# Where two norm-related steps stand among the matmuls of a hybrid decoder trunk: the first GLA head's key transposes, and the first token group's post-norm roots

## The chip, the cores and the metric

The kernel runs on one core of a Trainium2 chip. The metric is the device time of one execution in microseconds (us). Each run is timed on its own; several runs of one kernel give a median and a range. One further execution was recorded by the hardware profiler, and all rows below come from it.

## The reference, cut to what matters

The kernel computes a two-layer decoder trunk over 512 tokens and 16 meta tokens (528 columns) with a model width of 1024, all in float32. Each layer is a half-step SwiGLU feed-forward net, a token mixer, and a second half-step feed-forward net. Each is normed on its way in and again on its way out:

```
h = h + 0.5 * rmsnorm(swiglu(rmsnorm(h, g[0]), ...), g[1])
hn = rmsnorm(h, g[2])
mix = gla_mixer(hn, ...)      # layer 0; layer 1: swa_mixer(hn, ...)
h = h + rmsnorm(mix, g[3])
h = h + 0.5 * rmsnorm(swiglu(rmsnorm(h, g[4]), ...), g[5])
```

The mixer of layer 0 is chunked gated linear attention (GLA) with 4 heads of key width 128 and value width 256. Its part that the change touches, for one head:

```
chunk_kv = einsum('bhnsd,bhnsv->bhndv', kf * exp(b_last - bcum), vf)
S_next   = dec_c[..., None] * S + kv_c          # a scan over the chunks
o = o_intra + einsum('bhncd,bhndv->bhncv', q_dec, states)
```

The keys that go into the state, `kf * exp(b_last - bcum)`, have to be transposed on TensorE before the product with the values. The mixer of layer 1 is sliding-window attention. Between the layers one key/value set is computed from the normed residual.

## The kernel before, in words

Activations lie transposed: the 1024 channels are 8 tiles of 128 partitions, the tokens are columns. `H[:, k]` is tile k of the residual, `Y[:, k]` tile k of a sublayer's output. The columns are handled in two groups: group 0 has 272 columns (256 in layer 1), group 1 has 256.

A float32 product is made of three matmuls in a faster format: weight and activation are each split into a high and a low part, and high x high, low x high and high x low are summed (`mm3s`). Each weight tile of 128x512 thus needs one copy on ScalarE (ACT) and one subtraction on VectorE (DVE) before it can be used: `split_part`, with lines 226 and 227 in the profile. An activation tile is split in the same way: `build`, lines 398 (ACT) and 399 (DVE), gives the tile `x_<name>_k`.

What follows each sublayer is the same chain at six places, called by their names: `l0m` (after the first feed-forward net), `l0f1` (after GLA; the profile drops the last digit and writes l0f), `kv`, `l1m`, `l1f1` (l1f in the profile), `out`.

- `out_steps` computes the eight output tiles, for group 0 first and then for group 1 where the last tiles are concerned. A finished tile is added to `Y` (line 560 on DVE, or 558 on ACT), squared on ACT (`sq_post`, line 375; the first, and the last of group 1, straight into a sum, `acc_post`, line 372), and the squares are summed on POOL (line 376).
- Then `Residual.run` of that group starts as a job of its own. It waits `yield 1.8` and calls `roots`: two matmuls with a matrix of ones add the sums over the partitions (`st_post_<name><group>`, on TensorE, PE), ACT takes the reciprocal root (line 357) and a square (line 358), DVE refines it in three steps (lines 359 to 361).
- Then for each k, DVE multiplies by gain and root (line 437) and adds to `H` (line 438), ACT and DVE build `x_<name>_k`, ACT squares `H`. The roots of this pre-norm (`acc_<name>`, `R_<name>`) are applied later, to the product.
- `x_first` multiplies the new tiles with the next four weights: all k of group 0, then all k of group 1. `x_units` goes on with the other weights.

In GLA, `core(h)` is the job of one head. It runs while PE works through the `x` products of the other projections. In order: two scans on DVE, value transposes (`pv`, `pm`), decays `d`, the state's keys `f` (line 883 to 886, the last of which finishes them), keys `c` for the crossing chunk, `yield STATE_KEYS`, the transposes of `f` (`pk`), then the score products `pa` and `pb`, the states `ps`, the outputs `po` and `pn`, and a norm of its own (`st_go`).

The order of the work is set when the program is written. Jobs are generators; `Flow` holds a clock that only matmuls advance (`mm`: columns / 2400 for the fast format), and a `yield d` puts the job back until the clock has gone on by `d`. `mm3s` lets due jobs emit their instructions after each three matmuls. So a `yield` fixes behind which matmul a job's next instructions stand on PE, and among which others on ACT, DVE and POOL. On the chip each engine takes its instructions in this order and waits for data at the head of its own queue. One matmul with 272 columns advances the clock by 0.113, one with 256 by 0.107.

Of the kernel before, what the change touches and what calls it, by code (L numbers as in the profile page):

```python
# [40 lines left out]
START = 1.0  # L41
SECOND = 6.0
STATE_KEYS = 1.5
SCORE = 0.8
WIN = 2 * P + META
STAGGER = 5.0
# [78 lines left out]
def trunk_kernel(ctx: ExitStack, tc, a, out):  # L125
# [18 lines left out]
    def ps(name):  # L144
        return pp.tile([P, 512], F32, tag="ps", name=name)
# [203 lines left out]
    def roots(sums, n, c, name, dst=None, dim=D):  # L349
        s = ps(f"st_{name}")  # L350
        for i, t in enumerate(sums):
            mm(s[:, :n], ones, t[:, :n], i == 0, i == len(sums) - 1)
        yield SUMMED
        if dst is None:
            dst = (sums[1] if sums[1:] else acc_tile(f"root_{name}"))[:, :n]
        q, y = sums[0][:, :n], dst
        act.activation(y, s[:, :n], AF.Abs_reciprocal_sqrt, scale=1.0 / dim, bias=eps)
        act.activation(q, y, AF.Square, scale=dim ** -0.5)
        dve.scalar_tensor_tensor(q, s[:, :n], dim * 1e-6, q, op0=ALU.add, op1=ALU.mult)
        dve.tensor_scalar(q, q, -0.5 * c, 1.5 * c, op0=ALU.mult, op1=ALU.add)  # L360
        dve.tensor_tensor(y, q, y, op=ALU.mult)
        return y, s
# [57 lines left out]
    class Residual:  # L420
# [4 lines left out]
        def run(self, gi, g, sums):  # L425
            o, n = g
            nxt = self.nxt
            yield 1.8
            r, s = yield from roots(sums, n, self.c, f"post_{self.name}{gi}")
            if nxt is None:  # L430
                yield from self.store(gi, g, r)
                return
            for k in range(KD):
                h, y = H[:, k, o : o + n], Y[:, k, o : o + n]
                c = k % 2 * 256
                t = s[:, c : c + n] if n <= 256 else ps(f"t_{self.name}{gi}{k}")[:, :n]
                dve.scalar_tensor_tensor(t, y, self.gain(k), r, op0=ALU.mult, op1=ALU.mult)
                dve.tensor_tensor(h, t, h, op=ALU.add)  # L438
                nxt.build(gi, k)
                nxt.sumsq(gi, k)  # L440
                yield 1.0
            nxt.rjob[gi] = flow.spawn(nxt.factors(gi))
# [345 lines left out]
    def gla(x, finish):  # L788
        set_ahead(10)
        with tc.tile_pool(name="gp", bufs=1) as gp:  # L790
# [61 lines left out]
            def core(h, before):  # L852
# [39 lines left out]
                dve.tensor_tensor(kcv, kcv, blk(ks)[:, :, :64], op=ALU.mult)  # L892


                yield STATE_KEYS
                km = gp.tile([META, P], F32, tag="km", name=f"km{h}")
                p = ps(f"pk{h}")
                for b in range(3):
# [91 lines left out]
            for h in range(HEADS):  # L990
                cores.append(flow.spawn(core(h, [gate] + late + cores[h - 1 : h])))
                if h + 1 < HEADS:
                    kk = [("k", h + 1), ("q", h + 1), ("v", 2 * h + 2), ("v", 2 * h + 3)]
                    late = x_units(x, 4, L0, lambda i, g, p, kk=kk: evac(*kk[i], g, p))
# [71 lines left out]
    def swa(x, kv, finish):  # L1066
        kz, vt, vmz = kv
        set_ahead(10)
        with tc.tile_pool(name="ap", bufs=1) as ap:
# [25 lines left out]
            def soft(u, after):  # L1095
# [14 lines left out]
                for b in range(4):  # L1110
# [6 lines left out]
                    for e in range(2):  # L1117
# [3 lines left out]
                        )  # L1121
                    yield SCORE
                    for e in range(2):
# [242 lines left out]
```

## Time and profile before

| | |
|---|---|
| median of 3 runs | 1894.06 us (1893.08 to 1894.97) |
| the profiled execution, its time | 1895.05 us |
| the profiled execution, its span | 1893.3 us |
| mean granted TensorE clock | 0.995 |
| busy: PE / DVE / ACT / POOL | 1860.3 / 1356.2 / 1004.4 / 322.1 us |
| chain that ended last, PE's share | 84% |

The span runs from the first to the last recorded instruction; 1.75 us of the profiled execution's time lie around it. That execution took 0.99 us longer than the median. A row of the timeline gives a start in us from the span's start, a busy time in us, the engine, the line, the operation and the tile that it writes, and how many instructions stand together in the row; in square brackets stands how long the engine sat idle before it and which instruction ended that wait. The list of waits adds up these brackets by pair.

### The profile page before, as it was taken

The page shows a single profiled execution, that of the slowest core. Times are in us where ns is not written, and L with a number is a line of the kernel's source. Part 1 is how long each engine was busy: PE and PEld are TensorE (multiplying, and loading weights), DVE is VectorE, ACT ScalarE, POOL GpSimd, SP SyncE. Part 2 cuts the span into 40 slices and gives each one's busy share as a digit, 9 for nine tenths or more (in the row PEclk, how much of TensorE's full clock was granted, in tenths as well). Part 3 has the DMA queues.
Part 4 walks back from the last instruction along what each step waited for, and adds up shares of the span by engine and source line. Part 5 has one row for each costly group of instructions (what it writes and reads, how often), then busy time and mean ns, then how long its engine had stood idle before and what let it go on. Part 6 is the DMA issues. An engine that isn't in the chain of part 4 may idle for free.

```text
span 1893.3 us, 36987 instructions
## 1 busy us (share of the span) xinstructions
PE 1860.3 (98%) x14238; PEld 1775.4 (94%) x14238; DVE 1356.2 (72%) x2681; ACT 1004.4 (53%) x2181; POOL 322.1 (17%) x378
## 2 busy tenths in 40 slices
PE   8999999999999999999999999999989999999997
PEld 8999999998999999999999898989967898989897
DVE  6884848776574977484878775858788588858484
ACT  6662626563545665362655563636546566626363
POOL 2101010310001310101033001010353231010102
PEclk9999999999999999999999999999999999999999
DMA  5655556322123255555642456566321215565651
GB/s 192 151 153 138 151 145 168 106 71 72 49 65 104 68 134 156 141 153 139 169 148 57 106 153 154 151 150 171 109 67 35 79 46 127 155 153 156 151 146 45
DMA packets 133104, 231.17 MB, mean 122 GB/s; under 512 B 14912, under 2 KB 27584, under 8 KB 132928
## 3 DMA queue, kind: packets, MB, share of 16 engines
q1 hardware_dynamic: 111904, 190.94, 31.9%
q0 software_dynamic: 20736, 37.76, 12.8%
q8 instruction: 111, 1.82, 0.4%
q14 instruction: 65, 0.53, 0.1%
q10 hardware_dynamic: 288, 0.13, 0.0%
HBM read 226.67 MB, written 2.10 MB: 121 GB/s over the span
## 4 chain that ended last, share of the span: by engine, by line
PE 84%; DVE 11%; ACT 3%; issue 1%; DMA 0%; POOL 0%; SPq 0%; DVEq 0%; ACTq 0%; POOLq 0%
PE y L162 29%; PE a L162 21%; PE x L162 13%; PE c L162 10%; PE d L162 5%; DVE H L438 1%; PE o L162 1%; DVE w L227 1%; PE e L162 1%; PE po L162 1%; ACT w L226 1%; PE sc L162 1%; DVE x_l0m L399 1%; DVE x_l1f L399 1%; PE ps L162 0%
## 5 line engine op out<-in xcount | busy, mean ns | idle before, releaser
L252 POOL DMA_DIRECT2D raw<-in_w_in x144 | 125.7, 939 | 971.2 <-DMA raw<-in_w_in 331.6
L247 DVE TENSOR_TENSOR w_s<-raw,w_s 128x512 fp32r<-128x512 f32 x288 | 194.9, 688 | 105.6 <-ACT w_s L246 103.9
L162 PE MATMUL y<-hidl0f,w 128*128 128x256 f32 (+1 forms) x2112 | 260.5, 285 | 0.0
L162 PEld LDWEIGHTS y<-hidl0f,w 128*128 128x128 f32 x2112 | 258.7, 188 | 0.2
L227 DVE TENSOR_TENSOR w<-raw,w 128x512 fp32r<-128x512 f32 x378 | 242.9, 672 | 20.9 <-ACT w L226 18.9
L162 PE MATMUL y<-hidl1f,w 128*128 128x512 f32 (+1 forms) x1344 | 249.3, 346 | 0.5 <-ACT hidl1f L380 0.5
L162 PEld LDWEIGHTS y<-hidl1f,w 128*128 128x128 f32 x1344 | 212.2, 188 | 34.1 <-ACT hidl1f L380 1.3
L246 ACT ACTIVATE w_s<-raw 128x512 fp32r<-128x512 f32 x288 | 177.7, 625 | 108.2 <-DVE raw L262 67.7
L226 ACT ACTIVATE w<-raw 128x512 fp32r<-128x512 f32 x378 | 206.9, 586 | 33.8 <-PE y L162 26.5
L247 DVE TENSOR_TENSOR w<-raw,w 128x512 fp32r<-128x512 f32 x216 | 145.3, 688 | 37.7 <-ACT w L246 35.9
L162 PE MATMUL x<-x_l0m,w 128*128 128x272 f32 (+1 forms) x1200 | 158.7, 289 | 0.1
L246 ACT ACTIVATE w<-raw 128x512 fp32r<-128x512 f32 x216 | 130.3, 621 | 48.0 <-PE y L162 43.0
L560 DVE TENSOR_TENSOR Y<-y,Y 128x256 f32<-128x256 f32 (+2 forms) x176 | 82.1, 473 | 100.5 <-PE y L162 100.2
L162 PEld LDWEIGHTS x<-x_l0m,w 128*128 128x128 f32 x1200 | 149.8, 189 | 1.6 <-DVE x_l0m L399 0.3
L162 PE MATMUL a<-zl0f_t,w_s 128*128 128x264 f32 x864 | 117.3, 285 | 0.0
L162 PE MATMUL a<-zl1f_t,w_s 128*128 128x256 f32 x864 | 114.4, 281 | 0.8 <-ACT c L754 0.8
L376 POOL TENSOR_TENSOR acc_post<-acc_post,sq_post 128x256 f32<-128x256 f32 (+1 forms) x78 | 65.9, 845 | 286.2 <-ACT sq_post L375 283.9
L162 PEld LDWEIGHTS a<-zl0f_t,w_s 128*128 128x128 f32 x864 | 110.2, 188 | 0.0
L162 PEld LDWEIGHTS a<-zl1f_t,w_s 128*128 128x128 f32 x864 | 106.9, 188 | 1.9 <-ACT c L754 1.7
L162 PE MATMUL x<-x_l0f,w 128*128 128x256 f32 (+1 forms) x768 | 98.8, 289 | 7.9 <-ACT w L226 5.8
L162 PEld LDWEIGHTS x<-x_l0f,w 128*128 128x128 f32 x768 | 96.4, 191 | 9.4 <-ACT w L226 5.8
L162 PE MATMUL x<-x_l1f,w 128*128 128x256 f32 (+1 forms) x576 | 93.0, 320 | 1.5 <-ACT x_l1f L398 1.5
(369 smaller groups left out, 3337.3 us busy)
## 6 DMA issues: line engine op xcount, KB each, us to landing
raw<-in_w_in SPq DMA_DIRECT2D x424, 256.0 KB, 3.7
raw<-in_w_in POOLq DMA_DIRECT2D x144, 256.0 KB, 5.2
raw<-in_w_out SPq DMA_DIRECT2D x96, 256.0 KB, 3.5
raw<-in_gla_in SPq DMA_DIRECT2D x50, 256.0 KB, 3.2
raw<-in_w_last SPq DMA_DIRECT2D x48, 256.0 KB, 3.5
raw<-in_w_out SPq DMA_DIRECT2D x64, 128.0 KB, 3.0
raw<-in_gla_out SPq DMA_DIRECT2D x16, 256.0 KB, 2.9
raw<-in_w_q SPq DMA_DIRECT2D x16, 256.0 KB, 4.1
```

The costliest lines, as they stand in the source:

```text
L162: inst = pe.matmul(o, lhs, rhs, start=start, stop=stop, skip_group_check=onto)
L226: act.activation(w[:, 0, :m], raw[:, :m], AF.Copy)
L227: dve.tensor_tensor(w[:, 1, :m], raw[:, :m], w[:, 0, :m].bitcast(F32), op=ALU.subtract)
L246: act.activation(w[:, 0, :512], src, AF.Copy)
L247: dve.tensor_tensor(w[:, 1, :512], src, w[:, 0, :512].bitcast(F32), op=ALU.subtract)
L252: pool.dma_start(dst, src, accum_op=ALU.add)
L376: pool.tensor_tensor(sums[0][:, :n], sums[0][:, :n], t[:, :n], op=ALU.add)
L399: dve.scalar_tensor_tensor(x[:, 1, o : o + n], h, self.gv(k), x[:, 0, o : o + n].bitcast(F32), op0=ALU.mult, op1=ALU.subtract,)
L438: dve.tensor_tensor(h, t, h, op=ALU.add)
L560: dve.tensor_tensor(y, p[:, :n], y, op=ALU.add)
```

## The change

A second constant is added, and two `yield`s take another value in one case each. Head 0 of GLA waits 5.5 units of the planner's clock ahead of its key transposes, where the other heads keep 1.5. At the six places, the job of group 0 waits 2.8 units ahead of its roots, where group 1 keeps 1.8. No instruction is added or taken away; the jobs that follow, and what shares the engines with them, stand elsewhere in the order.

```diff
 STATE_KEYS = 1.5
+FIRST_KEYS = 5.5
...
         def run(self, gi, g, sums):
             o, n = g
             nxt = self.nxt
-            yield 1.8
+            yield 1.8 if gi else 2.8
             r, s = yield from roots(sums, n, self.c, f"post_{self.name}{gi}")
...
-                yield STATE_KEYS
+                yield STATE_KEYS if h else FIRST_KEYS
                 km = gp.tile([META, P], F32, tag="km", name=f"km{h}")
                 p = ps(f"pk{h}")
                 for b in range(3):
                     transpose(p[:, b * P : (b + 1) * P], blk(kf)[:, b])
```

After the change every line of the kernel has a number higher by one. In the orders below a row gives the line, the operation, what it writes, what it reads, its size, and how many alike stand together; trailing numbers only tell buffers apart. The first place is PE around head 0's key transposes `pk0`: `x64` and `x65` are the sums of two successive units of projection weights, `f0` the head's keys. Before:

```order
L162 MATMUL x64_0_5403<-x_l0m_7_4773,w63_1_5211 128x272 x3
L162 MATMUL x64_1_5404<-x_l0m_7_4773,w63_1_5211 128x256 x3
L174 MATMUL pk0_5446<-ident_73,f0_5379 128x128 x3
L174 MATMUL pk0_5446<-ident_73,f0_5379 16x128
L162 MATMUL x65_0_5484<-x_l0m_0_4602,w64_0_5241 128x272 x3
L162 MATMUL pa0_5489<-d0_5378 128x128 x4
L162 MATMUL pb0_5490<-d0_5378,c0_5380 64x64 x4
```

And after:

```order
L163 MATMUL x64_1_5404<-x_l0m_7_4782,w63_1_5211 128x256 x3
L163 MATMUL x65_0_5472<-x_l0m_0_4611,w64_0_5241 128x272 x3
L163 MATMUL x65_1_5473<-x_l0m_0_4611,w64_0_5241 128x256 x3
L163 MATMUL x65_0_5472<-x_l0m_1_4636,w64_0_5241 128x272 x3
L163 MATMUL x65_1_5473<-x_l0m_1_4636,w64_0_5241 128x256 x3
L163 MATMUL x65_0_5472<-x_l0m_2_4662,w64_0_5241 128x272 x3
L163 MATMUL x65_1_5473<-x_l0m_2_4662,w64_0_5241 128x256 x3
L163 MATMUL x65_0_5472<-x_l0m_3_4683,w64_0_5241 128x272 x3
L175 MATMUL pk0_5496<-ident_73,f0_5379 128x128 x3
L175 MATMUL pk0_5496<-ident_73,f0_5379 16x128
```

Twenty-one matmuls of `x65` now stand ahead of `pk0`; `pa0` follows 18 matmuls behind `pk0` where it was 3.

The second place is ACT after GLA, around the root of group 0 at `l0f1`: `y89` is the last unit of output weights, `Y<-y89_3_272` takes over tile 3 of group 1, and the table load stands ahead of the reciprocal root. Before:

```order
L375 ACTIVATE sq_post89_7_0_7473<-Y_71 128x272
L357 ACT_TABLE_LOAD
L357 ACTIVATE acc_root_post_l0f10_7533<-st_post_l0f10_7498,eps_75 128x272
L558 ACTIVATE Y_71<-y89_3_272_7476 128x256
L358 ACTIVATE acc_post82_0_0_7161<-acc_root_post_l0f10_7533 128x272
L375 ACTIVATE sq_post89_3_1_7504<-Y_71 128x256
```

And after:

```order
L376 ACTIVATE sq_post89_7_0_7473<-Y_71 128x272
L559 ACTIVATE Y_71<-y89_3_272_7476 128x256
L376 ACTIVATE sq_post89_3_1_7502<-Y_71 128x256
L358 ACT_TABLE_LOAD
L358 ACTIVATE acc_root_post_l0f10_7547<-st_post_l0f10_7516,eps_75 128x272
L359 ACTIVATE acc_post82_0_0_7161<-acc_root_post_l0f10_7547 128x272
```

The takeover of tile 3 and its square now stand ahead of the table load and the root.

The third place is ACT at `l1f1`, up to the last tile of group 1 (`x_l1f1_7`); `w225` and `w226` are weights being split, `gu` and `hidl1f1` belong to the next feed-forward net's gate. Before:

```order
L398 ACTIVATE x_l1f1_6_18683<-H_70,vec_72 128x256
L375 ACTIVATE sq_l1f1_272_6_18893<-H_70 128x256
L380 ACTIVATE hidl1f1_0_18646<-gu_18870 128x256
L226 ACTIVATE w225_0_18896<-raw225_0_18810 128x512
L226 ACTIVATE w225_1_18899<-raw225_512_18812 128x512
L615 ACTIVATE gu_18914<-gu_18914 128x256
L398 ACTIVATE x_l1f1_7_18706<-H_70,vec_72 128x256
```

And after:

```order
L399 ACTIVATE x_l1f1_6_18698<-H_70,vec_72 128x256
L376 ACTIVATE sq_l1f1_272_6_18887<-H_70 128x256
L616 ACT_TABLE_LOAD
L616 ACTIVATE gu_18895<-gu_18895 128x256
L399 ACTIVATE x_l1f1_7_18718<-H_70,vec_72 128x256
```

The two splits of `w225`, which now stand ahead of group 1's first tile, and the gate's second step no longer stand between tile 6 and tile 7; the table load and the gate's first step, which stood ahead of tile 6, now do.

## The prediction

> **What bounds the kernel.** I began with the page: span, busy shares, clock, and the chain that ended last.
>
> ```profile
> span 1893.3 us, 36987 instructions
> PE 1860.3 (98%) x14238; PEld 1775.4 (94%) x14238; DVE 1356.2 (72%) x2681; ACT 1004.4 (53%) x2181; POOL 322.1 (17%) x378
> PEclk9999999999999999999999999999999999999999
> PE 84%; DVE 11%; ACT 3%; issue 1%; DMA 0%; POOL 0%; SPq 0%; DVEq 0%; ACTq 0%; POOLq 0%
> ```
>
> TensorE is busy for 1860.3 of 1893.3 us at an even, full clock. The change adds no matmul and takes none away, so all it can move is the remaining 33.0 us of PE's idleness. The list of waits on PE says where that lies.
>
> ```profile
> PE x L162 <- ACT w L226: 5.8, 1, 5.8
> PE pk L174 <- DVE f L886: 2.5, 1, 2.5
> PE x L162 <- ACT x_l1m L398: 1.9, 1, 1.9
> PE x L162 <- ACT x_l1f L398: 1.5, 2, 1.2
> PE x L162 <- DVE x_l1m L399: 1.1, 2, 0.8
> PE st_post_l0m L162 <- ACT acc_post L372: 0.4, 1, 0.4
> PE x L162 <- ACT x_l0f L398: 0.3, 1, 0.3
> PE x L162 <- DVE x_kv L399: 0.3, 1, 0.3
> PE x L162 <- DVE x_l0f L399: 0.3, 1, 0.3
> PE st_post_kv L162 <- POOL acc_post L376: 0.2, 1, 0.2
> ```
>
> The columns are the total, the number of waits and the longest. The 5.8 us are the program's start, which nothing here touches. The second row is one wait of 2.5 us: a `pk` for its keys. The others belong to the norm chains at the six places. So the change acts on one wait of 2.5 us and on 6.0 us of small ones.
>
> **Head 0's key transposes.** The timeline at the wait, PE and then DVE (the keys' last step and a weight split):
>
> ```profile
> 418.65 8.29 PE L162 MATMUL x<-x_l0m,w 128*128 128x272 f32 x66
> 429.49 0.70 PE L174 MATMUL pk<-ident,f 128*128 128x128 f32 x4 [2.55 <-DVE f L886]
> 428.88 0.56 DVE L886 TENSOR_TENSOR f<-f,qk 128x400 f32<-128x400 f32 x1
> 410.33 0.68 DVE L227 TENSOR_TENSOR w<-raw,w 128x512 fp32r<-128x512 f32 x1
> ```
>
> PE had run out of products at 429.49 - 2.55 = 426.94; the keys were done at 428.88 + 0.56 = 429.44. A product takes 8.29 / 66 = 0.126 us, so the 21 that now stand ahead of `pk0` fill 2.64 us and end at 429.58, 0.14 us after the keys. Their operands are there: `x_l0m` has been in use for whole units, and the last split of their weight `w64` is the last row, done at 411.01. The wait goes whole: **-2.55 us**. Bounds: not over 2.55, and nothing if a new wait takes its place (a rival below); as nothing holds the 21 products up, I take the whole.
>
> What is late next: everything behind `pk0` in head 0, and through it heads 1 to 3, comes later among the products. PE works through more of them in that time, so a delay costs only where the products run out. Head 1 and the end of head 3 show the cover:
>
> ```profile
> 454.82 6.43 PE L162 MATMUL x<-x_l0m,w 128*128 128x256 f32 x51
> 461.09 0.60 PE L174 MATMUL pk<-ident,f 128*128 128x128 f32 x4
> 543.88 1.05 PE L162 MATMUL st_go<-acc_go,ones 128*128 128x272 f32 x4
> 544.59 7.65 PE L162 MATMUL x<-x_l0m,w 128*128 128x272 f32 x60
> 587.74 16.53 PE L162 MATMUL y<-og,w 128*128 128x272 f32 x132
> ```
>
> Head 1's `pk` stands behind 51 products and doesn't wait. The last head's norm starts at 543.88 and its output is first read 40 us later, so the few us by which the heads' steps slip (four units of the planner's clock at most, some 36 products or 4.5 us) stay hidden: 0. Without that cover each us of slip would cost a us.
>
> **The roots of group 0.** One unit more is three calls of three matmuls; the row below gives 14.90 / 123 = 0.121 us for one, so `st_post` of group 0 comes 9 x 0.121 = 1.09 us later at each of six places. On PE the move itself costs nothing, since `y` products take its place. What can cost is the chain behind it: DVE and ACT build group 0's tiles later, and group 1's `st_post` and tiles queue behind. I follow the places one by one.
>
> `l0m`, PE's products and then ACT at the root, then DVE, ACT and PE at group 1's sum:
>
> ```profile
> 357.07 14.90 PE L162 MATMUL y<-hidl0f,w 128*128 128x256 f32 x123
> 357.55 1.28 ACT L357 ACT_TABLE_LOAD   x1
> 358.85 0.49 ACT L357 ACTIVATE acc_root_post_l0m<-st_post_l0m,eps 128x272 f32<-128x272 f32 x1
> 375.88 0.41 DVE L560 TENSOR_TENSOR Y<-y,Y 128x256 f32<-128x256 f32 x1
> 376.80 0.40 ACT L372 ACTIVATE acc_post<-Y 128x256 f32<-128x256 f32 x1
> 377.26 0.70 PE L162 MATMUL st_post_l0m<-acc_post,ones 128*128 128x256 f32 x2 [0.42 <-ACT acc_post L372]
> ```
>
> The table load hides most of the shift of `st_post`: the root can't start before 358.83 anyway. But one square now slips ahead of line 358, about 0.4 us, and up to 1.09 if `st_post` lands last. From there DVE runs without a break up to the last takeover of `Y` at 375.88, and PE already waits 0.42 us for what follows it. So the lateness reaches PE nearly whole: between 0 and 1.09, and I take **+0.7**, nearer the upper end, since no slack shows in the row.
>
> `l0f1`, where ACT's order changes most:
>
> ```profile
> 606.82 0.43 ACT L375 ACTIVATE sq_post<-Y 128x272 f32<-128x272 f32 x1
> 607.27 1.28 ACT L357 ACT_TABLE_LOAD   x1
> 609.26 0.49 ACT L357 ACTIVATE acc_root_post_l0f<-st_post_l0f,eps 128x272 f32<-128x272 f32 x1 [0.71 <-PE st_post_l0f L162]
> 609.64 0.38 ACT L558 ACTIVATE Y<-y 128x256 f32<-128x256 f32 x1
> 610.37 0.44 DVE L359 SCALAR_TENSOR_TENSOR acc_post<-st_post_l0f,acc_post 128x272 f32<-128x272 f32 x1 [22.85 <-ACT acc_post L358]
> 624.72 0.42 ACT L372 ACTIVATE acc_post<-Y 128x256 f32<-128x256 f32 x1
> 624.83 1.06 PE L162 MATMUL st_post_l0f<-acc_post,ones 128*128 128x256 f32 x4
> ```
>
> Before, the table load ran while ACT had nothing else and was over 0.71 us before the sum came. Now the takeover of tile 3 (about 609.3 to 609.6) and its square (to 610.0) go first, so the load ends at 610.0 + 1.28 = 611.3 and the root starts 2.0 us later than at 609.26. DVE, idle for 22.85 us ahead of its first step, starts 2.0 later with it. Group 1's `st_post` waits for the square at 624.72, which shares ACT with the late tiles: between 0 (ACT has gaps enough to catch up) and 1.3. Against that stand the two waits of 0.3 for group 1's tiles, ahead of which two weight splits now stand no longer: -0.6 to 0. I take **+0.6** in all, about the middle of the first.
>
> Here the Trainium skill would make it dearer: its page "ScalarE: Activation LUTs", section "What ACT_TABLE_LOAD costs", gives about 1.28 us for the load and about 1.38 us more for a drain at each switch. The trace has the 1.28, but at `l0m` the root starts 0.02 us after the load (357.55 + 1.28 to 358.85) and no drain shows. By the page the root would start 3.4 us later instead of 2.0, and the sum would be 1.4 higher, if all of it came through; the row decides.
>
> `l1f1`, DVE's last update of `H`, ACT, and PE:
>
> ```profile
> 1548.09 0.42 DVE L438 TENSOR_TENSOR H<-st_post_l1f,H 128x256 f32<-128x256 f32 x1
> 1549.20 1.14 ACT L226 ACTIVATE w<-raw 128x512 fp32r<-128x512 f32 x2
> 1550.81 0.49 ACT L398 ACTIVATE x_l1f<-H,vec 128x256 fp32r<-128x256 f32 x1
> 1551.35 3.06 PE L162 MATMUL x<-x_l1f,w 128*128 128x256 f32 x18 [1.25 <-ACT x_l1f L398]
> ```
>
> Tile 7's `H` is there at 1548.51, yet ACT reads it at 1550.81, because two splits (1.14 us) stand in between. These move ahead of group 1's first tile, but a table load of 1.28 us moves in, and group 0 ends up to 1.09 later on a DVE that both groups fill. Between -1.25 and +1.09; I take 0. At `kv`, `l1m` and `out` the same work stands in nearly the same order ahead of group 1's last tile: 0 each, between minus what the list of waits has there and +1.09.
>
> **Sum.** -2.55 + 0.7 + 0.6 = -1.25 us on the profiled execution's 1895.05 us (span 1893.3 and 1.75 around it), which gives 1893.8. That execution lies 0.99 above the median of 1894.06, so against the median I forecast 1894.06 - 1.25 = **1892.8 us**. A measurement of this kernel can tell about 0.2%, 3.8 us, from no change; the forecast lies within.
>
> **Rivals.**
>
> *The chains of group 1 gain.* At `l0f1` and `l1f1` splits leave the place ahead of tile 7. If the later start of group 0 clears ACT's and DVE's queues at the right time at all places, half of the waits on `x_l1m`, `x_l1f`, `x_l0f` and `x_kv` goes: (1.9 + 1.5 + 1.1 + 0.3 + 0.3 + 0.3) / 2 = 2.7, and the losses of 0.7 and 0.6 don't come. Then 1894.06 - 2.55 - 2.7 = 1888.8. For it: at `l1f1` ACT's queue, not the data, holds tile 7. Against it: at `l1m` DVE appears among the releasers too, and the same amount of work stays on it.
>
> *The lateness goes through everywhere.* Group 0's chain shares DVE with group 1, and PE reaches group 1's tiles just in time. If each place passes on its 1.09, and `l0f1` its 2.0, at the five places ahead of `out`, that is 4 x 1.09 + 2.0 = 6.4, and the time 1894.06 - 2.55 + 6.4 = 1897.9: slower. It decides from 6.35 us of passed lateness on. Against it: `st_post` at `l0f1` shows no bracket and so has some slack, and PE has hardly any wait at `kv`.
>
> *The wait moves on.* Head 0's transposes no longer wait, but a later step does (`ps` for the copies of `pk`, or DVE's drains of products that PE now makes earlier), and of the 2.55 us nothing is left. Then 1894.06 + 1.3 = 1895.4. For it: DVE made the keys late, and it still has the same queue. Against it: no later step of heads 0 to 3 shows a wait now.
>
> **Chances and range.** The forecast 0.42 (1890.3 to 1894.5), group 1's gain 0.33 (1887.5 to 1890.3), lateness throughout 0.14, the wait moves on 0.11. Faster by over 0.2% takes the second and a sliver of the first, 0.36; slower takes the third and a sliver of the fourth, 0.16; 0.48 remains. The range leaves out most of the third case and the far end of the second: 1887.8 to 1897.2. As both signs are in it, the likeliest case's own range stands above.
>
> **What the profile after would show.** The bracket at head 0's `pk` under 0.2 us, and none over 0.3 at its `pa`, `ps` and `po`; at `l0m` the bracket of `st_post` at about 1.1 in place of 0.42; at `l0f1` the root 2 us later against `st_post`'s neighbours, and a bracket ahead of group 1's `st_post`; the bracket of 1.25 at `l1f1` and that of 1.9 at `l1m` about as before. I would be wrong if the brackets on `x` tiles at the norm chains together fell or rose by more than 2.5 us, or if a new wait appeared in heads 1 to 3.

## The result, and the profile after

The changed kernel takes 1899.61 us (median of 8 runs, 1899.11 to 1901.38), the kernel before 1894.81 us (median of 8 runs, 1893.08 to 1895.33) beside it. The ratio is 1.0027 with a 95% interval of 1.0016 to 1.0037: slower by 4.8 us, where 1.25 us less was forecast. The profiled execution took 1899.64 us with a span of 1897.8 us, 4.5 us more than before; PE is busy for 1861.0 us against 1860.3. So the loss is mostly waiting: PE's idle time grew from 33.0 to 36.8 us, although the wait for `pk` is gone. The list of waits on PE after the change, the larger of its rows at the places of the change:

```profile
PE x L163 <- ACT x_l1f L399: 2.2, 2, 1.4
PE x L163 <- DVE x_l0f L400: 2.0, 1, 2.0
PE x L163 <- ACT x_l1m L399: 1.9, 1, 1.9
PE st_post_l0m L163 <- POOL acc_post L377: 1.4, 1, 1.4
PE st_post_kv L163 <- POOL acc_post L377: 1.2, 1, 1.2
PE y L163 <- ACT hidl1f L381: 1.1, 1, 1.1
PE st_post_l1m L163 <- POOL acc_post L377: 1.1, 1, 1.1
PE x L163 <- DVE x_l1m L400: 0.7, 2, 0.4
```

The row of 2.5 us for `pk` is gone. In its place stand three waits of 1.1 to 1.4 us for POOL at group 1's sum (0.4, 0.2 and none before), one of 2.0 at `l0f1`, and more at `l1f1`.

**The keys gained more than their wait.** PE around head 0's transposes, before:

```profile
430.68 1.91 PE L162 MATMUL pa<-d 128*128 128x128 f32 x8
432.52 1.06 PE L162 MATMUL pb<-d,c 128*64 128x64 f32 x8
```

and after:

```profile
419.95 10.85 PE L163 MATMUL x<-x_l0m,w 128*128 128x272 f32 x87
430.79 0.66 PE L175 MATMUL pk<-ident,f 128*128 128x128 f32 x4
433.46 1.05 PE L163 MATMUL pa<-d 128*128 128x128 f32 x8
434.45 0.68 PE L163 MATMUL pb<-d,c 128*64 128x64 f32 x8
```

There is no bracket at `pk`, as forecast. But the same eight products `pa` take 1.05 us where they took 1.91, and `pb` 0.68 where it took 1.06. The busy time of the engines by stretches of 5 us says why; the columns behind POOL's are the granted clock, the share of the DMA engines, and GB/s. Before, then after:

```profile
425.00:430.00 5.00, 2.45 (x22) 2.23 (x21) 5.00 (x12) 1.60 (x4) 0.00 (x0) 1.00 0.34 107
430.00:435.00 5.00, 5.00 (x33) 4.53 (x31) 2.56 (x7) 2.56 (x5) 0.00 (x0) 0.66 0.37 107
```

```profile
425.00:430.00 5.00, 5.00 (x43) 5.00 (x42) 5.00 (x12) 2.79 (x7) 0.00 (x0) 1.00 0.33 105
430.00:435.00 5.00, 5.00 (x45) 4.64 (x43) 4.20 (x10) 2.68 (x6) 0.00 (x0) 1.00 0.51 147
```

In the kernel before, the granted clock falls to 0.66 in the 5 us behind the pause of 2.55 us; afterwards it stays at 1.00. Stretches that begin where the drop begins show its true shape, again for the kernel before:

```profile
426.59:430.00 3.41, 0.86 (x9) 0.65 (x8) 3.41 (x9) 1.36 (x3) 0.00 (x0) 1.00 0.15 55
430.00:433.41 3.41, 3.41 (x21) 3.19 (x19) 2.06 (x5) 2.56 (x5) 0.00 (x0) 0.50 0.53 154
433.41:436.83 3.42, 3.42 (x23) 2.71 (x21) 0.98 (x4) 0.00 (x0) 0.00 (x0) 1.00 0.01 2
```

The clock is halved for one stretch of 3.41 us. The stretch ahead of it holds the whole pause: PE is busy there for 0.86 us of 3.41. The Trainium skill's page "TensorE: Matmul & The Clock Gate" (Part 1, What's actually happening) has the gate fall to half the clock after one idle window of about 3.4 us. The trace agrees on the half and on the length; but 2.55 us of idleness in such a stretch were enough here, so the measurement decides.

**What the later roots cost at `l1m`.** This place had been put down at nothing. ACT, POOL and PE at group 1's sum, before:

```profile
1364.97 0.42 ACT L375 ACTIVATE sq_post<-Y 128x256 f32<-128x256 f32 x1 [0.27 <-POOL acc_post L376]
1365.79 0.73 POOL L376 TENSOR_TENSOR acc_post<-acc_post,sq_post 128x256 f32<-128x256 f32 x1
1367.70 1.02 PE L162 MATMUL st_post_l1m<-acc_post,ones 128*128 128x256 f32 x4
```

and after:

```profile
1366.20 0.51 ACT L399 ACTIVATE x_l1m<-H,vec 128x256 fp32r<-128x256 f32 x1 [0.69 <-DVE H L439]
1366.62 0.40 ACT L376 ACTIVATE sq_l1m<-H 128x256 f32<-128x256 f32 x1
1366.93 0.40 ACT L376 ACTIVATE sq_post<-Y 128x256 f32<-128x256 f32 x1
1367.16 0.73 POOL L377 TENSOR_TENSOR acc_l1m<-acc_l1m,sq_l1m 128x256 f32<-128x256 f32 x1 [0.79 <-ACT sq_l1m L376]
1367.85 0.72 POOL L377 TENSOR_TENSOR acc_post<-acc_post,sq_post 128x256 f32<-128x256 f32 x1
1368.63 1.13 PE L163 MATMUL st_post_l1m<-acc_post,ones 128*128 128x256 f32 x4 [1.10 <-POOL acc_post L377]
```

Each row is the last of its kind ahead of PE's sum, the square of tile 6. Before, POOL had added it at 1366.52, and PE came 1.2 us later. Afterwards it stands, on ACT and on POOL, behind one more step of group 0 (a tile and its square, which wait for DVE); it ends at 1368.57, 2.05 us later, and PE waits.

### The profile page after: what moved, and what is told of

Same layout as the page of the kernel before. It is cut to its first block, busy times and chain, and to the rows that moved or that the text cites. A ratio compares the mean times of both kernels' runs of the same rounds, so it can differ in the third digit from the quotient of the medians.

```text
span 1897.8 us, 36994 instructions
## 1 busy us (share of the span) xinstructions
PE 1861.0 (98%) x14238; PEld 1775.1 (94%) x14238; DVE 1359.0 (72%) x2681; ACT 1004.4 (53%) x2181; POOL 322.9 (17%) x378
## 4 chain that ended last, share of the span: by engine, by line
PE 82%; DVE 13%; ACT 3%; issue 1%; DMA 0%; POOL 0%; SPq 0%; DVEq 0%; ACTq 0%; POOLq 0%
PE y L163 28%; PE a L163 21%; PE x L163 13%; PE c L163 9%; PE d L163 5%; DVE H L439 1%; DVE w L228 1%; PE o L163 1%; PE e L163 1%; PE po L163 1%; PE sc L163 1%; DVE x_l1f L400 0%; DVE x_l0m L400 0%; DVE st_post_l1m L438 0%; PE ps L163 0%
```

## The experiments

All times are medians; each ratio is against runs of the kernel before on the same chip, 1894.1 to 1894.8 us. Where nothing else is said, an edit is made in the changed kernel.

### One part alone

Keys alone:

```diff
-            yield 1.8 if gi else 2.8
+            yield 1.8
```

> Only head 0's key transposes moved (5.5 units), roots as before. Theory 1 (the wait of 2.55 us goes, and so do the slower matmuls behind it, where the granted clock of the kernel before shows 0.66 from 430 to 435 us): 3.8 us less than before, about 1891.0 us, granted clock 1.00 throughout 425 to 440. Theory 2 (only the wait goes): 2.55 less, about 1892.3. Theory 3 (the slip of the other heads costs later): 0 to 1 less, about 1894.

Measured: 1890.95 us, ratio 0.9982 (0.9974 to 0.9991); granted clock 1.00 in every stretch from 420 to 445 us. The median is the 3.8 us of theory 1, but the interval, 1.7 to 4.9 us, would allow the 2.55 of theory 2 too. The recordings decide. The rows `x<-zeros` and `d<-zeros` are matmuls that clear a sum; they stand at the same steps of PE's work in every kernel. From the one at group 1's first product at `l0m` to that at `l0f1`, with GLA in between (386.13 and 634.10 us in the kernel before), PE takes 248.0 us before and 248.2 with the roots alone, but 244.2 to 244.6 in ten of the twelve recordings with the keys at 5.5 (244.9 and 245.8 in the two below that are without POOL's add or with earlier roots). So 3.4 to 4.0 us go, more than the wait: theory 1 holds.

Roots alone:

```diff
-FIRST_KEYS = 5.5
+FIRST_KEYS = 1.5
```

> Only group 0's roots moved (2.8 units), head 0's key transposes as before. Theory 1: the loss is all here and adds to the other part: about 1899.6 + 3.8 = 1903.4 us. Theory 2 (the gain of the keys is 2.55): 1902.1. Theory 3 (the loss comes from the two parts together): under 1899.

Measured: 1903.71 us, ratio 1.0052 (1.0039 to 1.0064), with `pk`'s bracket of 2.55 back and 0.66 as the clock of the 5 us behind it. The two parts add: 3.8 us gained, 8.7 to 9.0 lost. The interval reaches down to 1902.1, theory 2's time; what speaks for theory 1 is the slower clock, which is back.

### How much of the keys' delay is needed

```diff
-FIRST_KEYS = 5.5
+FIRST_KEYS = 3.5
...
-            yield 1.8 if gi else 2.8
+            yield 1.8
```

> Head 0's key transposes moved by half as much (3.5 units): 10 products stand ahead of them in place of 21, roots as before. They fill 10 x 0.126 = 1.26 us, so a wait of 1.3 us stays. If the slower clock follows any pause: half of the wait gained, about 1893.5 us, and a granted clock under 0.9 in one stretch of 5 us. If it follows only a pause that is long enough: 1.26 + 1.25 = 2.5 less, 1892.3, clock 1.00.

Measured: 1893.39 us, ratio 0.9995 (0.9986 to 1.0004).

The same with 4.5:

> Head 0's key transposes at 4.5 units, behind 12 products in place of 21; roots as before the change. A wait of 2.55 - 12 x 0.126 = 1.04 us stays. If a pause of this length brings the slower clock in some executions: between 1892 and 1893.4 in the median. If never: 1890.95 + 1.04 = about 1892.0, clock 1.00 behind it.

Measured: 1893.51 us, ratio 0.9998 (0.9989 to 1.0007).

The same with 7.5:

> Head 0's key transposes at 7.5 units, behind 39 products, 2.3 us more than needed; roots as before the change. If the slip of the heads stays hidden: as with 5.5, about 1891 us and no new wait up to the output products. If the heads' chains run out of products or of PSUM: over 1892, with waits at pk, ps or po, or ahead of the output products.

Measured: 1891.43 us, ratio 0.9989 (0.9980 to 0.9998). The brackets at `pk` in these three, head 0's with 3.5 and with 4.5, and head 3's with 4.5 and with 7.5:

```profile
429.64 0.66 PE L175 MATMUL pk<-ident,f 128*128 128x128 f32 x4 [1.30 <-DVE f L887]
```

```profile
429.50 0.66 PE L175 MATMUL pk<-ident,f 128*128 128x128 f32 x4 [1.09 <-DVE f L887]
526.55 0.66 PE L175 MATMUL pk<-ident,f 128*128 128x128 f32 x4 [0.69 <-DVE f L887]
```

```profile
528.06 0.65 PE L175 MATMUL pk<-ident,f 128*128 128x128 f32 x4 [0.61 <-DVE f L887]
```

The brackets come as worked out (1.30 and 1.09 for 1.3 and 1.04), and with 7.5 the gain is complete and the slip hidden but for 0.61 us at head 3. The clock behind the shorter pauses is 1.00 in both recordings, which speaks for a pause that has to be long enough. In the recordings PE takes 246.0 and 246.5 us for GLA, 1.5 and 2.0 more than with the keys alone, and that is the brackets: 1.30 and 0.21 for 3.5, and 1.09, 0.16 and 0.69 (heads 0, 1 and 3) for 4.5. The medians lie 2.4 and 2.6 us above the keys alone, which the intervals don't tell from 1.5 and 2.0. Whether a pause of 1.3 us brings the slower clock in some of the runs that were not recorded stays open.

### Half the shift, and the other way

```diff
-            yield 1.8 if gi else 2.8
+            yield 1.8 if gi else 2.3
```

> The changed kernel with half the shift of group 0's roots (2.3 in place of 2.8). Theory 1 (a lateness that passes on in proportion): half of the loss of 8.7 us, about 1895.2 us. Theory 2 (steps of the order: one instruction more or less ahead of group 1's sums): nearly the whole loss or nearly none, so about 1899 or about 1891.

Measured: 1898.65 us, ratio 1.0025 (1.0015 to 1.0036). Half the shift costs 7.7 of the 8.7 us: steps of the order (theory 2), not a lateness that passes on in proportion. The waits say the same at four of the five places, where they are as with the whole shift (1.4 at `l0m`, 1.9 at `l0f1`, 1.2 at `kv`, 1.3 ahead of the first tile at `l1f1`); only at `l1m` the wait for POOL is 0.4 in place of 1.1.

```diff
-            yield 1.8 if gi else 2.8
+            yield 1.8 if gi else 0.8
```

> Head 0's key transposes at 5.5 units, and group 0's roots one unit earlier than before (0.8 in place of 1.8). If the chains behind group 0's roots pass their lateness on in both directions: group 1's waits of 6.0 us shrink by 2 to 4, about 1888 us. If 1.8 is at the point where earlier brings nothing (the root then waits for its sums): as with the keys alone, about 1891. If the earlier sums make PE wait for the squares: over 1892.

Measured: 1903.16 us, ratio 1.0047 (1.0033 to 1.0060): earlier is worse than later, 12.2 us above the keys alone. Two of its rows, group 0's and group 1's sum at `l0m`:

```profile
357.05 0.72 PE L163 MATMUL st_post_l0m<-acc_post,ones 128*128 128x272 f32 x2 [0.54 <-POOL acc_post L377]
379.57 1.13 PE L163 MATMUL st_post_l0m<-acc_post,ones 128*128 128x256 f32 x4 [1.91 <-POOL acc_post L377]
```

PE now comes to group 0's sum before POOL has it (about 0.5 us at each of the six places), and group 1's sum waits as well. The third case of the expectation, then; the roots can go wrong in both directions.

### POOL's part

```diff
-        if i == 0 or apart and i == count - 1:
+        if i == 0 or apart and i >= count - 2:
...
-        return sm.tile([P, 272], F32, tag="acc", name=f"acc_{name}", bufs=6)
+        return sm.tile([P, 272], F32, tag="acc", name=f"acc_{name}", bufs=7)
```

> The changed kernel, but the squares of tile 6 of group 1 at each of the six places get a sum of their own on ACT, as tile 7's already do, so that POOL no longer adds them and the sum over the partitions takes three matmuls in place of two (0.13 to 0.27 us more on PE at each place, 0.8 to 1.6 in all). Theory 1 (POOL's queue, where the sum of tile 6 now stands behind the pre-norm's sums, makes group 1's roots wait): the waits of 1.42, 1.17 and 1.10 us for POOL at l0m, kv and l1m fall to 0.5 or less, about 1898 us in all. Theory 2 (DVE and ACT make the tiles late, and POOL is only the last in line): the waits stay, now for ACT, at about 0.9 to 1.4, and the time rises to about 1900.5.

Measured: 1895.90 us, ratio 1.0011 (1.0002 to 1.0020), 3.7 us less than the changed kernel by the medians and 3.0 by the ratios, although it has more matmuls. The sums of group 1 at `l0m`, `kv` and `l1m`:

```profile
377.63 0.70 PE L163 MATMUL st_post_l0m<-acc_post,ones 128*128 128x256 f32 x2 [0.21 <-ACT acc_post L373]
...
987.15 1.75 PE L163 MATMUL st_post_kv<-acc_post,ones 128*128 128x256 f32 x6
...
1365.86 1.46 PE L163 MATMUL st_post_l1m<-acc_post,ones 128*128 128x256 f32 x6
```

The waits of 1.42, 1.17 and 1.10 are at 0.21 and none, so they went through POOL's add of tile 6, and theory 2 is out. The edit takes away the add and its place in POOL's queue together, so it doesn't say which of the two counts. Nor does the lateness begin on POOL. At `l1m`, in the rows further up, the square of tile 6 already starts 1.96 us later on ACT, of the 2.05 by which POOL ends later. At `l0m` it is 0.98 on ACT and 1.63 on POOL, before and then after:

```profile
374.28 0.42 ACT L375 ACTIVATE sq_post<-Y 128x256 f32<-128x256 f32 x1 [0.47 <-POOL acc_post L376]
375.14 0.95 POOL L376 TENSOR_TENSOR acc_post<-acc_post,sq_post 128x256 f32<-128x256 f32 x1
```

```profile
375.26 0.40 ACT L376 ACTIVATE sq_post<-Y 128x256 f32<-128x256 f32 x1
377.00 0.72 POOL L377 TENSOR_TENSOR acc_post<-acc_post,sq_post 128x256 f32<-128x256 f32 x1
```

The time fell by more than was expected. Of the 3.5 us between the two recorded spans, 1.8 lie in the attention of layer 1, where this recording has one stretch of 3.41 us at half the clock (from 1422 us) and the changed kernel's has three; the next section shows such differences without this edit.

### One place at a time

Each with the later roots at one place, here `l0m`:

```diff
-            yield 1.8 if gi else 2.8
+            yield 2.8 if gi == 0 and self.name == "l0m" else 1.8
```

> Head 0's keys at 5.5, and the later roots at l0m alone. If the places add up, each with the waits that it shows: 1890.95 + 1.0 = about 1892.0 us, with the wait for POOL at group 1's sum at 1.4. If the places work on each other: 1891 or over 1893.

> Head 0's keys at 5.5, and the later roots at l0f1 alone. If the places add up: the wait for tile 7 of group 1 at 1.96 us in place of 0.32, about 1890.95 + 1.7 = 1892.7 us. If the lateness of this place came down from l0m: about 1891.

> Head 0's keys at 5.5, and the later roots at kv alone. If the places add up: the wait for POOL at group 1's sum at 1.17 us in place of 0.22, and 0.2 at a group 0 tile: about 1890.95 + 1.2 = 1892.2 us. If kv costs nothing by itself: about 1891.

> Head 0's keys at 5.5, and the later roots at l1m alone. If the places add up: the wait for POOL at group 1's sum at 1.1 us, one of the waits for tiles down by 0.4, and the slower clock behind it as in the changed kernel or not: 1890.95 + 0.7 to 1.8, 1891.7 to 1892.7 us. With l0m (2.1), l0f1 (1.8), l1f1 and a like share for kv the places then make up the 8.7 us. If not: under 1891.3, and the loss is one of the places together.

> Head 0's keys at 5.5, and the later roots at l1f1 alone. If the places add up: the new wait of 1.4 us ahead of group 1's first tile, the one at tile 7 down from 1.2 to 0.8, the wait for the first gate up by 0.6: about 1890.95 + 1.7 = 1892.7 us. If that wait was handed down from the places ahead: about 1891.

The table compares them with the keys alone (1890.95 us). Beside the medians stands PE's time between the two rows `zeros` around the place; around `l0m` these are, with the keys alone and then with the later roots at `l0m` (the other pairs start at 631.45 and 690.90, 884.34 and 1020.80, 1359.85 and 1372.94, 1522.46 and 1595.12 us with the keys alone):

```profile
275.44 0.29 PE L163 MATMUL d<-zeros 128*128 128x264 f32 x1
386.95 0.63 PE L163 MATMUL x<-zeros 128*128 128x512 f32 x2
```

```profile
275.31 0.29 PE L163 MATMUL d<-zeros 128*128 128x264 f32 x1
387.86 0.62 PE L163 MATMUL x<-zeros 128*128 128x512 f32 x2
```

| place | us, ratio | median more | PE around the place, us | its brackets |
|---|---|---|---|---|
| `l0m` | 1893.07, 0.9994 (0.9986 to 1.0003) | 2.1 | 112.55 for 111.51 | sum of group 1 at 1.43 for 0.42 |
| `l0f1` | 1892.73, 0.9994 (0.9985 to 1.0003) | 1.8 | 61.08 for 59.45 | tile 7 at 1.96 for 0.32 |
| `kv` | 1893.14, 0.9995 (0.9986 to 1.0004) | 2.2 | 137.77 for 136.46 | sum of group 1 at 1.16 for 0.22, a tile at 0.21 |
| `l1m` | 1892.52, 0.9990 (0.9981 to 0.9999) | 1.6 | 14.39 for 13.09 | sum of group 1 at 1.10, a tile at 0.43 for 0.86 |
| `l1f1` | 1894.45, 1.0000 (0.9991 to 1.0009) | 3.5 | 75.06 for 72.66 | first tile 1.44, tile 7 0.79 for 1.23, the gate 1.11 for 0.46 |

Every place shows alone the waits that it has in the changed kernel, so none was handed down from another. The medians add up to 11.2 us, with an interval of some 0.09% (1.7 us) on either side of each ratio, and can't tell the sizes. PE's times can: in these five recordings and that of the keys alone, a place with the same roots takes the same time within 0.1 us (the one difference found elsewhere is 0.5 us, at `l0f1` with the splits held back). With the later roots the times are 1.0, 1.6, 1.3, 1.3 and 2.4 us longer, 7.7 in all; in the changed kernel the same rows give 1.0, 1.7, 1.3, 1.3 and 2.4, 7.8 in all, of the 8.7 by which its median lies above the keys alone. So the places add up. (The spans are no measure here: the recorded execution of the keys alone reached its first row `zeros` at 22.59 us, that of the kernel before at 21.78, and both do the same work up to there.)

Behind `l1m` this doesn't work, in the attention of layer 1, with group 1's tiles ahead of it. There the recordings of kernels that don't differ from the keys alone at `l1m` lie between 148.7 and 150.4 us, with 149.5 for the keys alone, and hold two or three stretches of 3.41 us at half the clock. The changed kernel's 150.3 us lie within that, so its further 0.8 us there can't be put down to the change.

### The weight split at `l1f1`

As `l1f1` alone, with the two splits held back:

```diff
     def split_unit(i, raws):
-        yield 2.2
+        yield 3.2 if i == 225 else 2.2
```

> As the run with the later roots at l1f1 alone, but the two splits of weight w225, which had moved ahead of group 1's first tile, are held back until behind its tile 7 (their job waits 3.2 units in place of 2.2; they are needed behind tile 7 alone). Theory 1 (the splits, 1.8 us on DVE, make group 1's first tile late): the wait of 1.4 us ahead of that tile falls under 0.3, and the time to about 1891.3 us. Theory 2 (the later root by itself makes it late): the wait stays over 1, the time at about 1892.7.

Measured: 1894.46 us, ratio 1.0000 (0.9991 to 1.0009), no less than `l1f1` alone. PE at group 1's first tile and behind its last:

```profile
1537.41 1.31 PE L163 MATMUL x<-x_l1f,w 128*128 128x256 f32 x9 [0.31 <-ACT x_l1f L399]
...
1552.57 0.50 PE L163 MATMUL x<-x_l1f,w 128*128 128x512 f32 x1 [1.26 <-ACT w L227]
```

The wait ahead of the first tile fell from 1.44 to 0.31, as theory 1 has it, but the next product then waits 1.26 us for the split itself. The splits did make the first tile late; yet they have to be done on ACT and DVE before PE is through with group 1, and moving them only moved the wait.

With the keys alone, where the job of the two splits waits 4.0 units in place of 2.2:

> Head 0's keys at 5.5, the roots as before the change, and the two splits of w225 held back (4.0 units in place of 2.2) until behind group 1's tile 7 at l1f1, for which ACT then no longer stands behind them. If those splits cost PE the wait of 1.23 us for tile 7: about 0.8 to 1.2 less than with the keys alone, 1889.9 us. If the next product then waits for the splits instead: about 1891.

Measured: 1891.18 us, ratio 0.9981 (0.9973 to 0.9990). In its profile the wait of 1.23 us for tile 7 is at 0.16, with 0.39 ahead of the next product, and PE takes 71.7 us around `l1f1` for 72.7: the gain that was expected. The median shows none of it over 1890.95; a us lies within the intervals. This kernel and the keys alone are faster than both kernels compared here; between them the runs don't decide.

## Why the prediction was wrong, point by point

- *Head 0's key transposes, -2.55 us.* The mechanism and the wait were right: no bracket at `pk`, and none at head 0's `pa`, `ps` and `po`. The term was too small: alone it measured 3.8 us, and 3.4 to 4.0 in PE's time for GLA. What it left out is the halved clock behind the pause, which a view by stretches of the profile before showed. The prediction had read "an even, full clock" from the page's 40 slices, which hold 47 us each and show 9 throughout.
- *The slip of heads 1 to 3, 0.* Right: even 2 units more (7.5) gave 1891.43 us.
- *`l0m`, +0.7.* The size was near (1.0 in the bracket and in PE's time, 2.1 in the median), the cause was not: PE waits for the sum with tile 6, through ACT and POOL, not for DVE's takeover of tile 7. The run without POOL's add of tile 6 showed it.
- *`l0f1`, +0.6.* Alone it measured 1.8 us in the median and 1.6 in PE's time. The root did start 1.7 us behind the start of group 0's sum where it was 0.66 before, and that sum itself came 1.09 later among PE's products: about the 2.0 us of the working. No bracket came at group 1's sum. But the waits for group 1's tiles, which were to shrink by up to 0.6, grew to 1.96. DVE's part of tile 7, the changed kernel's row first, then that of the keys alone:

```profile
641.72 0.43 DVE L382 TENSOR_TENSOR hidl0f<-gu,hidl0f 128x272 fp32r<-128x272 f32 x1
642.07 0.68 DVE L228 TENSOR_TENSOR w<-raw,w 128x512 fp32r<-128x512 f32 x1
642.67 0.43 DVE L620 TENSOR_TENSOR gu<-gu 128x272 f32<-128x272 f32 x1
643.02 1.21 DVE L228 TENSOR_TENSOR w<-raw,w 128x512 fp32r<-128x512 f32 x1
644.16 0.43 DVE L382 TENSOR_TENSOR hidl0f<-gu,hidl0f 128x272 fp32r<-128x272 f32 x1
644.51 0.47 DVE L400 SCALAR_TENSOR_TENSOR x_l0f<-H,vec,x_l0f 128x256 fp32r<-128x256 f32 x1
```

```profile
642.64 0.47 DVE L400 SCALAR_TENSOR_TENSOR x_l0f<-H,vec,x_l0f 128x256 fp32r<-128x256 f32 x1
```

  Two splits had left the place ahead of tile 7, but two others and the gate's steps still stood there on a DVE that had started later: it was done 1.9 us later, at much the same position of PE. No run took these splits away, so that they, and not only DVE's later start, hold tile 7 is argued from the rows.
- *`kv`, `l1m` and `out`, 0 each.* This is the step that failed, and `l1f1` below with it: the terms put at 0. The roots came to 0.7 + 0.6 = 1.3 us in the sum and measured 7.8; of the 6.5 between, 2.4 are `l1f1`, 1.3 each `kv` and `l1m`, and 1.4 `l0m` and `l0f1`. The prediction compared the work ahead of group 1's last tile; what moved stands ahead of group 1's *sum*. There the square of tile 6 slipped behind one more step of group 0 on ACT and POOL. At `l1m` it came 2.05 us later, beyond the upper bound of 1.09, since the square lost the whole step that it slipped behind, with that step's own wait. Alone, `kv` and `l1m` measured 1.3 us each in PE's time (2.2 and 1.6 in the medians). Only `out` was right (0.50 for 0.49).
- *`l1f1`, 0 between -1.25 and +1.09.* It measured 2.4 us in PE's time (3.5 in the median), the dearest of the six. The wait at tile 7 did shrink (1.25 to 0.80), as its row promised, but the splits, gone from there, cost 1.45 us ahead of the first tile, a place that the working didn't look at. Nor were they alone ahead of tile 7: the gate's second step stood there too (1550.49 to 1550.91 us on ACT).
- *The rivals.* The one on the other side, lateness through everywhere, came nearest: 1897.9 forecast and 1899.6 measured, with 0.14 as its chance. It had the places right, and the mechanism only in part: half the shift costs nearly as much, and at three of the five places the wait is for the sum with tile 6, over ACT and POOL, which it didn't name. The gain of group 1's chains came at single tiles alone (0.4 at `l1m`, 0.45 at `l1f1`), and the wait of the keys didn't move on: none appeared in the heads. The sign that was given, 2.5 us more or less on `x` tiles, only just showed (5.4 to 7.9); 3.1 us more of waiting stand at group 1's sums, for which no sign was given but at `l0m` and `l0f1`.
- *The table load.* After the change the root at `l0f1` started 0.01 us after the end of the load (608.91 and 608.92 us), at `l0m` before it was 0.02: the switch took its 1.28 us and no more.

The difference between the two spans, 4.5 us, is found by the rows `zeros`: -3.4 us in GLA, +1.0 at `l0m`, +1.1 at `l0f1` (which the keys alone make 0.6 shorter), +1.0 at `kv`, +1.3 at `l1m`, +0.8 in the attention behind it and +2.4 at `l1f1` make 4.2. The last 0.3 are spread over the rest, most of it in steps that the keys alone show too.

## What to carry to other kernels

Where an order is fixed in advance, follow a moved job on every queue that it shares, up to each place where the bound engine waits for that queue, the small sums included; an instruction there can lose not the shift but the whole step that it slips behind. A pause of the bound engine can cost more than its length: look at the granted clock in stretches of a few us behind it. Where medians can't tell a us, the time between two rows that stand at the same step in both profiles can. And a gain and a loss in one change are worth separating, since the gain alone (0.9982) was there to be had.

## What was not expected of the hardware

A pause of 2.55 us on TensorE was followed by half the granted clock for 3.41 us, in the two recordings with that pause; in the thirteen others without a pause there the clock stays at 1.00 from 420 to 445 us, and in the two with pauses of 1.30 and 1.09 us as well.

In all recordings, from the program's first 15 us to its last 20, every drop is to 0.50 and lasts 3.41 us or twice that; and the drops of one recording lie a whole number of 3.41 us apart (430.0 and 1392.5 us in the kernel before: 282 times). In GLA and at `l0f1`, what counted is how much of a pause fell into one such stretch. With 2.55, 2.13 and 1.94 us of idleness in it the next one was at half the clock (before; roots alone; half the shift); with 1.76 and less it wasn't. So the wait of 1.9 to 2.0 us at `l0f1` lowered the clock in the recording with half the shift, where one stretch holds nearly all of it (PE then takes 62.6 us around the place for 61.1), and not in the changed kernel's, nor in that with `l0f1` alone, where it is divided over two. These are 17 recordings; where between 1.76 and 1.94 us the limit lies, and whether it is one, is not shown.
